# A third buffer for the scan's decay rows, four ScalarE operations held behind others, and other PSUM banks and an early Silu table at the entry of the second layer

## The chip, the cores and the metric

The kernel runs on one core of a Trainium2 chip. The metric is the device time of one execution in microseconds (us). Three executions of the kernel before took 1940.17, 1943.55 and 1943.87 us; their median is 1943.55 us. The profiled execution is a fourth one: it took 1941.21 us, of which 1939.4 us lie between its first and its last instruction (its span). All work is in float32; a matrix product that needs full precision is made of three products of a high and a low part of each factor.

## The reference, cut to what matters

One inference step of a trunk of two layers, for a prompt of 1024 positions and a sample group of 8 x 8 positions. The width is 1024. The first layer is a Mamba-2 SSD mixer with 8 groups of 4 heads, the second is a latent attention (MLA) over 16 heads with a Silu gate.

```python
def reference(...):
    for i in range(DEPTH):                       # DEPTH = 2
        ln = rms_norm(h, norm_w[i])
        if i % 2 == 0:                           # SSD: project, convolve, scan, gate, project
            out = ssd_mixer(ln, ...)
        else:                                    # MLA: project, attend, gate, project
            out = mla_output(o, gate, mla_w_out)
        h = h + out
    y = rms_norm(h, final_norm_w)

def ssd_scan(x, dt, a_head, bm, cm, init_state):   # chunks of 128 positions, per group
    a_cs = cumsum(dt * a_head)
    decay = where(causal, exp(a_cs[l] - a_cs[s]), 0)
    y_diag = einsum(cb * decay, x * dt)            # inside a chunk
    y_off = einsum(cc, state) * exp(a_cs)          # from the chunks before
    return y_diag + y_off, final_state

def mla_output(o, gate, w_out):
    return (o * silu(gate)) @ w_out
```

## The kernel before, in words

**Tiling.** The 1088 positions are nine row tiles: 0 to 7 with 128 prompt positions each, and 8 with the 64 sample positions. Activations that feed a projection are kept transposed as a high and a low part (`xh`, `xl` in the first layer, `hh`, `hl` in the second), eight slices of 128 channels each.

**First layer.** For each of the 8 groups g there are two pieces of work. The projection of group g (class `Group`, lines 481 to 572) makes four convolution blocks (`pj` in PSUM, `raw`, `acc`), applies Silu, and then the gates: nine products `pz` that ScalarE copies into `z`, a tile for row tiles 0 to 4 and another for 5 to 8, and Silu over each of them (lines 569, 571, 572). The scan of group g (`ssd_chunks`, lines 580 to 670) walks the nine row tiles. For each it loads the decay rows into a tile `M` of 128 x 4 x 128 by a DMA from `acs_d` (line 627), adds the causal mask on VectorE (line 628), takes four exponentials on ScalarE (line 631), multiplies with `cb` = B times C on VectorE (line 632), and multiplies with the transposed inputs `xsT` on TensorE (`py`, line 636). Beside it the states go on (`st`, `S`, `Ch`, `Sh`), and `ssd_states` handles the sample group in four further steps; it takes two tiles `xr` out of the same ring of buffers as `M` (line 688), and line 724 copies part of the product `pv` into `yo`. The ring has two buffers.

The scan of group g runs beside the projection of group g + 1. The last scan, g = 7, has no next group and runs beside the output projection (`OutHalf`, `ssd_out`): the first half of the weights (`xh`, `xl` again, made from `wor`/`wraw` at lines 769 and 770), row tiles `yta` transposed to `ytpa`, split by ScalarE (`yha`, line 127) and VectorE (`yla`, line 133), and multiplied into `poa`. In names such as `M7_0`, `yha0` or `z70` the first digit of a scan tile is the group, the last one the row tile. The second half of the output projection is `pob`; its result is added into the rows `xrb` on VectorE (lines 851 and 853, the second for the sample tile).

**Entry of the second layer** (`mla_in`). The rows are scaled, transposed into `xtp` (line 268) in groups of three row tiles, and split into `hh` by ScalarE (line 273) and `hl` by VectorE (line 274). Beside the transposes the first two of eight gate blocks are projected (`gate_block`): `pj` gets 24 products per piece of positions, and ScalarE applies Silu into `gt` (line 972). The weights of a block are loaded by DMA, copied to `wgh` on ScalarE (line 127) and split into `wgl` on GpSimd (line 131); the ring of weights has three buffers. The PSUM tiles of the second layer come from a new pool, laid out in the order in which its tags are first used: `tr` (three banks, for `xtp`), `pj` (two), `y` (three). They lie over the banks of the first layer's pool, whose first banks are those of `pj`, which `pob` used last.

**The end.** `pieces` (lines 1891 to 1965) makes the last projection, adds it to the rows `h`, takes the sum of squares per row on ScalarE (line 1935 for the sample tile), joins the partial sums on VectorE (lines 1939 and 1949), scales by 1/1024 and adds epsilon (line 1950), takes the power -1/2 on GpSimd (line 1951) and scales the rows.

**What sets the order.** Almost the whole program is written in a natural order, and a list scheduler with a model of the chip's times puts the instructions of each engine into a fixed order, so a constraint or a buffer more at one place can move instructions at others. `tc.issue_after(x)` tells it that what follows is to come after instruction x. The heads of the attention and what follows on TensorE and GpSimd have an order written by hand. Each engine takes its own instructions strictly in the order that stands in the program, and a wait holds up all that is behind it on that engine.

## Time and profile before

| what | value |
|---|---|
| time, three runs | 1940.17, 1943.55, 1943.87 us (median 1943.55) |
| profiled execution | 1941.21 us, span 1939.4 us, mean granted TensorE clock 0.996 |
| TensorE busy | 1895.6 us, 98% of the span |
| VectorE, ScalarE, GpSimd busy | 1192.2 us (61%), 1109.9 us (57%), 837.5 us (43%) |
| table loads of ScalarE for the decay rows (line 631) | 28, 1.28 us each |

In a row of the timeline stand start and length in us, engine, line, operation, output and inputs, and in brackets the idle time of the engine ahead of it with what ended it; the length runs from the first start to the last end of the merged instructions. In a row of the waits stand who waited for whom, the sum in us, the number of waits and the longest. In a row of a stretch stand, for each engine, busy time and number of instructions, then the granted TensorE clock (1.00 is full), the share of the DMA engines and their rate.

### The profile page before, as it was taken

The page shows a single profiled execution, that of the slowest core. Times are in us where ns is not written, and L with a number is a line of the kernel's source. Part 1 is how long each engine was busy: PE and PEld are TensorE (multiplying, and loading weights), DVE is VectorE, ACT ScalarE, POOL GpSimd, SP SyncE. Part 2 cuts the span into 40 slices and gives each one's busy share as a digit, 9 for nine tenths or more (in the row PEclk, how much of TensorE's full clock was granted, in tenths as well). Part 3 has the DMA queues.
Part 4 walks back from the last instruction along what each step waited for, and adds up shares of the span by engine and source line. Part 5 has one row for each costly group of instructions (what it writes and reads, how often), then busy time and mean ns, then how long its engine had stood idle before and what let it go on. Part 6 is the DMA issues. An engine that isn't in the chain of part 4 may idle for free.

```text
span 1939.4 us, 33638 instructions
## 1 busy us (share of the span) xinstructions
PE 1895.6 (98%) x12023; PEld 1730.3 (89%) x12023; DVE 1192.2 (61%) x2501; ACT 1109.9 (57%) x2535; POOL 837.5 (43%) x1122
## 2 busy tenths in 40 slices
PE   9999999999999999899999999999999999899998
PEld 7999999999999999788787998898888888788887
DVE  5567666656666666765533104476887888766674
ACT  6467666666666676732214314336777777855552
POOL 2446565555655555443003212103443334764551
PEclk9999999999999999999999999999999999989999
DMA  5123323332323332544433333133111112654431
GB/s 168 47 72 89 98 82 94 83 108 85 97 81 96 86 93 88 193 157 159 179 116 118 123 152 94 56 107 96 47 51 41 51 41 59 215 167 155 156 128 39
DMA packets 181087, 202.02 MB, mean 104 GB/s; under 512 B 18828, under 2 KB 147608, under 8 KB 180536
## 3 DMA queue, kind: packets, MB, share of 16 engines
q1 hardware_dynamic: 175864, 180.08, 30.1%
q0 software_dynamic: 4976, 19.66, 3.0%
q8 instruction: 95, 1.56, 0.3%
q14 instruction: 72, 0.59, 0.1%
q10 hardware_dynamic: 80, 0.13, 0.0%
HBM read 146.52 MB, written 53.28 MB: 103 GB/s over the span
## 4 chain that ended last, share of the span: by engine, by line
PE 88%; DVE 3%; DMA 3%; ACT 3%; issue 1%; POOL 1%; SPq 0%; POOLq 0%; DVEq 0%; ACTq 0%
PE pj L86 21%; PE pz L98 9%; PE pq L98 6%; PE pob L98 5%; PE p L98 5%; PE poa L98 4%; PE py L636 3%; PE sc L86 3%; PE o L86 2%; PE sc L1369 2%; PE o L1432 2%; PE o L1434 2%; PE st L1401 2%; PE st L1402 2%; PE st L1403 2%; PE o L1433 2%
## 5 line engine op out<-in xcount | busy, mean ns | idle before, releaser
L86 PE MATMUL pj<-xh,wih 128*128 128x384 f32 (+1 forms) x768 | 254.2, 335 | 0.9 <-ACT xh L273 0.5
L86 PE MATMUL pj<-xl,wih 128*128 128x384 f32 (+1 forms) x768 | 254.0, 331 | 0.0
L86 PE MATMUL pj<-xh,wil 128*128 128x384 f32 (+1 forms) x768 | 253.2, 330 | 0.0
L1415 POOL TENSOR_TENSOR tl<-P,th 128x384 fp32r<-128x384 f32 (+1 forms) x96 | 90.6, 944 | 232.5 <-ACT P L1413 190.9
L526 DVE SCALAR_TENSOR_TENSOR acc<-raw,vec,acc 128x1112 f32<-128x1112 f32 x96 | 141.6, 1476 | 25.9 <-ACT acc L522 24.9
L86 PEld LDWEIGHTS pj<-xh,wih 128*128 128x128 f32 x768 | 143.9, 188 | 2.5 <-ACT xh L273 1.1
L86 PEld LDWEIGHTS pj<-xl,wih 128*128 128x128 f32 x768 | 144.5, 188 | 1.0
L86 PEld LDWEIGHTS pj<-xh,wil 128*128 128x128 f32 x768 | 144.4, 188 | 0.5
L98 PE MATMUL pz<-wih,xh 128*128 128x256 f32 x504 | 142.9, 287 | 0.9 <-ACT z L567 0.8
L98 PE MATMUL pz<-wil,xh 128*128 128x256 f32 (+1 forms) x504 | 140.4, 285 | 0.9 <-DVE wil L133 0.9
L1412 ACT ACTIVATE th<-st 128x512 fp32r<-128x512 f32 x192 | 94.6, 493 | 66.0 <-PE st L1408 50.3
L631 ACT ACTIVATE M<-M,tok 128x128 f32<-128x128 f32 (+1 forms) x288 | 91.0, 386 | 67.2 <-DVE M L628 66.9
L98 PE MATMUL pz<-wih,xl 128*128 128x256 f32 x448 | 128.2, 286 | 0.0
L1705 POOL TENSOR_TENSOR kvl<-pgr,kvh 128x256 fp32r<-128x256 f32 x128 | 96.5, 781 | 60.5 <-ACT kvh L1703 60.3
L98 PEld LDWEIGHTS pz<-wih,xh 128*128 128x128 f32 x504 | 96.0, 190 | 2.0 <-ACT z L567 1.3
L98 PEld LDWEIGHTS pz<-wil,xh 128*128 128x128 f32 (+1 forms) x504 | 92.7, 184 | 1.7 <-DVE wil L133 1.1
L1413 ACT ACTIVATE P<-st 128x512 f32<-128x512 f32 x192 | 93.5, 487 | 0.0
L628 DVE TENSOR_TENSOR M<-M,negu 128x512 f32<-128x512 f32 x64 | 53.2, 831 | 65.5 <-DMA M<-acs_d 65.1
L613 POOL TENSOR_TENSOR xdd<-xsT,tok 128x256 f32<-128x256 f32 x64 | 50.4, 788 | 84.1 <-ACT xsT L599 84.0
L133 DVE TENSOR_TENSOR wil<-wraw,wih 128x512 fp32r<-128x512 f32 x88 | 72.0, 825 | 23.6 <-ACT wih L127 20.4
L98 PEld LDWEIGHTS pz<-wih,xl 128*128 128x128 f32 x448 | 85.3, 190 | 0.1
L1415 DVE TENSOR_TENSOR tl<-P,th 128x512 fp32r<-128x512 f32 x96 | 70.7, 737 | 18.9 <-ACT P L1413 18.7
(832 smaller groups left out, 6299.0 us busy)
## 6 DMA issues: line engine op xcount, KB each, us to landing
wraw<-in_ssd_w_in SPq DMA_DIRECT2D x92, 256.0 KB
M<-acs_d SPq DMA_DIRECT2D x64, 256.0 KB
s<-in_state_ssm SPq DMA_DIRECT2D x32, 256.0 KB
y_d<-y SPq DMA_DIRECT2D x64, 128.0 KB
out_s_ssm<-s SPq DMA_DIRECT2D x32, 256.0 KB
wraw<-in_ssd_w_out SPq DMA_DIRECT2D x12, 512.0 KB
q_d<-qt SPq DMA_DIRECT2D x32, 192.0 KB
qp<-q_d SPq DMA_DIRECT2D x8, 768.0 KB
```

The lines of the kernel that those rows point to most:

```text
L86: nc.tensor.matmul(out, a, b, start=(i == 0), stop=(i == n - 1))
L98: nc.tensor.matmul(o, a, b, start=(j == 0), stop=(j == len(ops) - 1))
L133: return (eng or nc.vector).tensor_tensor(lo, src, hi.bitcast(F32), op=ALU.subtract)
L526: last = nc.vector.scalar_tensor_tensor(acc, raw[:, j : j + n], k.convw[j][:, blk : blk + 1], acc, op0=ALU.mult, op1=ALU.add)
L613: nc.gpsimd.tensor_tensor(v3(xdd), v3(xsT), hb(2), op=ALU.mult)
L628: nc.vector.tensor_tensor(M[:m, :, :m], M[:m, :, :m], (k.negs if smp else k.negu)[:m, :m].unsqueeze(1).to_broadcast([m, 4, m]), op=ALU.add)
L631: nc.scalar.activation(M[:m, h, :m], M[:m, h, :m], AF.Exp, bias=tk[:, 0, 4 * g + h : 4 * g + h + 1])
L636: nc.tensor.matmul(py[:m, h * 64 : h * 64 + 64], M[:m, h, :m], xsT[:m, h * 64 : h * 64 + 64], start=True, stop=True)
L1412: nc.scalar.activation(th[:, :n], ps[:, :n], AF.Exp, scale=SCALE)
L1413: nc.scalar.activation(P[:, :n], ps[:, :n], AF.Exp, scale=SCALE)
L1415: eng.tensor_tensor(tl[:, :n], P[:, :n], th[:, :n].bitcast(F32), op=ALU.subtract)
L1705: nc.gpsimd.tensor_tensor(rl[:, j], raw[:, j], rh[:, j].bitcast(F32), op=ALU.subtract)
```

## The change

Eight edits, which belong together in five groups:

1. The ring of buffers that holds `M` and `xr` in the scan gets three buffers (`bufs=3`).
2. Four operations of ScalarE are held behind others: in the projection of group 7, the Silu over `z70` behind the last copy into `yo` that stands before it; in the scan of group 7, the four exponentials of row tile 0 behind the last copy of the split of `ytpa`; the weight copies of gate blocks 3 and 4 behind the Silu of the third pieces of gate blocks 0 and 1.
3. At the entry of the second layer the Silu table is loaded by an instruction of its own ahead of the gate blocks.
4. The second layer's PSUM pool is opened with a tile of tag `y` first, so that `y` gets the first three banks, `tr` the next three and `pj` the last two.
5. For the sample tile at the end, the scale of 1/1024 goes into the square on ScalarE (by a scale of 1024 to the power -1/2), and epsilon into the addition at line 1939, so that line 1950 falls away there.

```diff
@@ def split
-    nc.scalar.copy(hi, src)
+    k.cast = nc.scalar.copy(hi, src)
@@ Group.gates
             if i == 4:
-                nc.scalar.activation(z, z, AF.Silu)
+                with k.tc.issue_after(k.yoc.ins) if g == G - 1 else nullcontext():
+                    nc.scalar.activation(z, z, AF.Silu)
@@ ssd_chunks
-        M = sp.tile([128, 4, 128], F32, tag="M", name="M" + tag, bufs=2)
+        M = sp.tile([128, 4, 128], F32, tag="M", name="M" + tag, bufs=3)
...
-        for h in range(4):
-            nc.scalar.activation(M[:m, h, :m], M[:m, h, :m], AF.Exp, bias=...)
+        with k.tc.issue_after(k.ycast.ins) if g == G - 1 and i == 0 else nullcontext():
+            for h in range(4):
+                nc.scalar.activation(M[:m, h, :m], M[:m, h, :m], AF.Exp, bias=...)
@@ ssd_states
-        xr = sp.tile([128, 4, 128], F32, tag="M", name=f"xr3{tag}{q}", bufs=2)[:, :3, :96]
+        xr = sp.tile([128, 4, 128], F32, tag="M", name=f"xr3{tag}{q}", bufs=3)[:, :3, :96]
...
-            nc.scalar.copy(yr, pv[32:64, :128])
+            k.yoc = nc.scalar.copy(yr, pv[32:64, :128])
@@ OutHalf.prep
             split(k, yh[:, qs, :m], yh[:, qs, 64:] if m == 64 else yl[:, qs], pv)
+            k.ycast = k.cast
@@ gate_block
-    ws = kslices(load_w(...), 8)
+    with k.tc.issue_after(k.gts[5].ins) if b in (3, 4) else nullcontext():
+        ws = kslices(load_w(...), 8)
...
-        k.nc.scalar.activation(gt[:, t0 : t0 + n], p[:, :n], AF.Silu)
+        k.gts.append(k.nc.scalar.activation(gt[:, t0 : t0 + n], p[:, :n], AF.Silu))
@@ mla_in
+            k.gts = []
+            tc.keep_in_program_order(nc.scalar.preload_act_table_set("silu_and_others"))
@@ pieces
-                    nc.scalar.activation(junk[:, c], h[:m, c], AF.Square, accum_out=ss[:m, hf : hf + 1])
+                    nc.scalar.activation(junk[:, c], h[:m, c], AF.Square, scale=D**-0.5, accum_out=ss[:m, hf : hf + 1])
...
-                        nc.vector.tensor_tensor(ss[:m, 0:1], ss[:m, 0:1], ss[:m, 1:2], op=ALU.add)
+                        nc.vector.tensor_scalar(ss[:m, 0:1], ss[:m, 0:1], ss[:m, 1:2], EPS, op0=ALU.add, op1=ALU.add)
...
-            nc.vector.tensor_tensor(r, ss[:m, 0:1], ss[:m, len(cs) - 1 : len(cs)], op=ALU.add)
-            nc.vector.tensor_scalar(r, r, 1.0 / D, EPS, op0=ALU.mult, op1=ALU.add)
+            if src:
+                nc.vector.tensor_tensor(r, ss[:m, 0:1], ss[:m, 2:3], op=ALU.add)
+            else:
+                nc.vector.tensor_tensor(r, ss[:m, 0:1], ss[:m, 1:2], op=ALU.add)
+                nc.vector.tensor_scalar(r, r, 1.0 / D, EPS, op0=ALU.mult, op1=ALU.add)
@@ layer_mla
+        k.psum.tile([128, 512], F32, tag="y", name="y2", bufs=PB["y"])
```

Since the order is the scheduler's, the edits move instructions elsewhere too. Three places follow. In the rows the digits after a tile's name are numbers of buffers; line numbers of the changed kernel are up to eleven higher than before.

ScalarE where the last scan begins, before: the second table load here is for the exponentials of the first decay tile of group 7.

```order
L571 ACTIVATE z75_10203<-z75_10203 128x768
L127 CAST Ch7_1_10550<-acc70_9057 128x128
L667 COPY fo6_7_10200<-pf6_7_10197 128x256
L599 COPY xsT6_8_10263<-trp6_8_10260 64x256
L631 ACT_TABLE_LOAD
L631 ACTIVATE M7_0_10410<-M7_0_10410,tok_73 128x128
L109 COPY z75_10203<-pz_10344 64x256
L631 ACTIVATE M7_0_10410<-M7_0_10410,tok_73 128x128 x3
L127 CAST yha0_10328<-ytpa00_10330 128x512
L660 ACTIVATE xD6_7_10163,yssq_72<-y6_7_10190 128x256
L127 CAST yha0_10328<-ytpa01_10337 128x512
```

The same place in the change:

```order
L572 ACTIVATE z75_10203<-z75_10203 128x768
L127 CAST yha0_10328<-ytpa00_10330 128x512
L127 CAST yha0_10328<-ytpa01_10337 128x512
L633 ACT_TABLE_LOAD
L633 ACTIVATE M7_0_10410<-M7_0_10410,tok_73 128x128 x4
L662 ACTIVATE xD6_7_10163,yssq_72<-y6_7_10190 128x256
L109 COPY z75_10203<-pz_10344 64x256
L600 COPY xsT7_0_10394<-trp7_0_10390 128x256
L127 CAST BTh7_0_10396<-trp7_0_10390 128x128
L127 CAST xddh7_0_10402<-xdd7_0_10400 128x256
```

Both copies `yha0` now stand ahead of the table load and of the four exponentials of `M7_0`, which stood ahead of them.

VectorE some 15 us later in the last scan, before, from the split `sl7_800` of the first sample state to the split of the transposed B of row tile 1 (`xl` are the low parts of the last two weight slices):

```order
L133 TENSOR_TENSOR sl7_800_10465<-s0p7_800_10459,sh7_800_10464 128x512
L770 SCALAR_TENSOR_TENSOR xl_99<-wraw_10382,vec_154,xh_98 128x8x128
L731 TENSOR_TENSOR s07_800_10457<-s07_800_10457,sn7_800_10480 128x512
L133 TENSOR_TENSOR yla1_10519<-ytpa10_10520,yha1_10518 128x512
L628 TENSOR_TENSOR M7_1_10562<-M7_1_10562,negu_69 128x512
L770 SCALAR_TENSOR_TENSOR xl_99<-wraw_10386,vec_154,xh_98 128x8x128
L725 TENSOR_TENSOR yo7_10438<-yo7_10438,pv7_800_10468 32x128
L628 TENSOR_TENSOR M7_2_10647<-M7_2_10647,negu_69 128x512
L133 TENSOR_TENSOR yla1_10519<-ytpa11_10527,yha1_10518 128x512
L816 TENSOR_SCALAR yta3_10867<-yta3_10867,yrsa_10319 128x256 x4
L133 TENSOR_TENSOR BTl7_1_10541<-trp7_1_10534,BTh7_1_10540 128x128
```

The same stretch in the change:

```order
L133 TENSOR_TENSOR sl7_800_10465<-s0p7_800_10459,sh7_800_10464 128x512
L629 TENSOR_TENSOR M7_2_10647<-M7_2_10647,negu_69 128x512
L733 TENSOR_TENSOR s07_800_10457<-s07_800_10457,sn7_800_10480 128x512
L629 TENSOR_TENSOR M7_3_10809<-M7_3_10809,negu_69 128x512
L133 TENSOR_TENSOR yla1_10519<-ytpa10_10520,yha1_10518 128x512
L727 TENSOR_TENSOR yo7_10438<-yo7_10438,pv7_800_10468 32x128
L133 TENSOR_TENSOR yla1_10519<-ytpa11_10527,yha1_10518 128x512
L634 TENSOR_TENSOR M7_1_10562<-M7_1_10562,cb7_1_10560 128x512
L772 SCALAR_TENSOR_TENSOR xl_99<-wraw_10382,vec_154,xh_98 128x8x128
L634 TENSOR_TENSOR M7_2_10647<-M7_2_10647,cb7_2_10645 128x512
L818 TENSOR_SCALAR yta3_10867<-yta3_10867,yrsa_10319 128x256 x4
L772 SCALAR_TENSOR_TENSOR xl_99<-wraw_10386,vec_154,xh_98 128x8x128
```

The last `xl` stood in the fifth row behind `sl7_800`; it now stands in the eleventh, behind the decay tiles 1 to 3 and the four scalings of `yta3`.

TensorE at the entry of the second layer, the last product `pob` of the first layer and the first transposes and products of the second, with the semaphores that each waits for. Before:

```order
L98 MATMUL pob_12435<-woh_11536,yhb_12368 128x512
L268 MATMUL xtp_0_12484<-ident,xt_11842 128x128 [waits DVE_49,PE_49]
L268 MATMUL xtp_0_12484<-ident,xt_11924 128x128
L268 MATMUL xtp_0_12484<-ident,xt_12006 128x128
L268 MATMUL xtp_1_12490<-ident,xt_11842 128x128
```

In the change:

```order
L98 MATMUL pob_12435<-woh_11536,yhb_12368 128x512
L268 MATMUL xtp_0_12486<-ident,xt_11842 128x128
L268 MATMUL xtp_0_12486<-ident,xt_11924 128x128
L268 MATMUL xtp_0_12486<-ident,xt_12006 128x128
L268 MATMUL xtp_1_12492<-ident,xt_11842 128x128
```

The order is the same; the first transpose no longer waits for VectorE.

More of the change, by code (lines that the diff above doesn't have):

```diff
@@ L629, in ssd_chunks @@
                                 (k.negs if smp else k.negu)[:m, :m].unsqueeze(1).to_broadcast([m, 4, m]), op=ALU.add)
-        for h in range(4):
-            nc.scalar.activation(M[:m, h, :m], M[:m, h, :m], AF.Exp, bias=tk[:, 0, 4 * g + h : 4 * g + h + 1])
+        with k.tc.issue_after(k.ycast.ins) if g == G - 1 and i == 0 else nullcontext():
+            for h in range(4):
+                nc.scalar.activation(M[:m, h, :m], M[:m, h, :m], AF.Exp, bias=tk[:, 0, 4 * g + h : 4 * g + h + 1])
         nc.vector.tensor_tensor(M[:m, :, :m], M[:m, :, :m],
@@ L967, in gate_block @@
 def gate_block(k, wp, raws, b):
-    ws = kslices(load_w(k, wp, k.I["mla_w_in"][0][:, 800 + 128 * b : 928 + 128 * b], 8, 128, "wg", 3, raws, eng=k.nc.gpsimd, sub=4), 8)
+    with k.tc.issue_after(k.gts[5].ins) if b in (3, 4) else nullcontext():
+        ws = kslices(load_w(k, wp, k.I["mla_w_in"][0][:, 800 + 128 * b : 928 + 128 * b], 8, 128, "wg", 3, raws,
+                            eng=k.nc.gpsimd, sub=4), 8)
     gt = wp.tile([128, T], F32, tag="gt", name=f"gt{b}", bufs=2)
     def ev(ci, t0, n, p):
-        k.nc.scalar.activation(gt[:, t0 : t0 + n], p[:, :n], AF.Silu)
+        k.gts.append(k.nc.scalar.activation(gt[:, t0 : t0 + n], p[:, :n], AF.Silu))
     for ci in range(3):
```

## The prediction

> **What bounds the kernel now.** I read the page's busy line, then the stretches of the span, then TensorE's waits in the stretches that lose time, and last the instructions around those waits. First the page and the stretches (TensorE's busy time is the second number of a row, the clock stands ahead of the last two):

> ```profile
> PE 1895.6 (98%) x12023; PEld 1730.3 (89%) x12023; DVE 1192.2 (61%) x2501; ACT 1109.9 (57%) x2535; POOL 837.5 (43%) x1122
> ...
> 40.00:770.00 730.00, 723.05 (x5239) 705.87 (x5238) 465.17 (x760) 477.12 (x1155) 403.18 (x590) 1.00 0.30 85
> 770.00:850.00 80.00, 73.32 (x487) 64.69 (x486) 53.84 (x100) 50.15 (x114) 35.97 (x48) 0.98 0.57 189
> 1035.00:1085.00 50.00, 46.34 (x274) 40.83 (x273) 20.43 (x39) 26.12 (x49) 25.54 (x34) 1.00 0.46 150
> 1640.00:1720.00 80.00, 67.92 (x409) 58.95 (x408) 58.62 (x118) 58.37 (x120) 61.06 (x72) 0.94 0.64 200
> 1918.00:1940.00 22.00, 13.89 (x94) 12.06 (x92) 11.71 (x35) 3.81 (x10) 1.08 (x2) 0.91 0.12 36
> ```

> TensorE is busy in 1895.6 of 1939.4 us and its instructions stay the same in number and kind, so only its 44 us of idle time and its slow stretches can change. The edits reach four stretches: groups 0 to 6 of the scan (40 to 770, idle 7.0 us), the last scan (770 to 850, 6.7), the entry of the second layer (1035 to 1085, 3.7) and the end (8.1). The 12.1 us idle at 1640 to 1720 lie in code that is not touched. TensorE's waits in the last scan and around it:

> ```profile
> PE poa L98 <- ACT yha L127: 1.5, 1, 1.5
> PE pv L722 <- DVE sl L133: 1.3, 2, 1.1
> PE cb L625 <- DVE yo L725: 1.0, 1, 1.0
> PE poa L98 <- DVE xl L770: 0.9, 1, 0.9
> PE pz L98 <- ACT z L567: 0.8, 1, 0.8
> PE st L86 <- DVE BTl L133: 0.6, 1, 0.6
> PE st L86 <- ACT xddh L127: 0.3, 1, 0.3
> PE st L86 <- POOL xddl L133: 0.2, 1, 0.2
> ```

> **The entry of the second layer.** These rows carry it, TensorE's first, then those of VectorE, ScalarE and GpSimd:

> ```profile
> 1042.60 1.17 PE L268 MATMUL xtp<-ident,xt 128*128 128x128 f32 x9 [1.59 <-DVE xrb L853]
> 1056.58 0.45 PE L86 MATMUL pj<-hh,wgh 128*128 128x384 f32 x1 [0.77 <-ACT gt L972]
> 1079.59 0.44 PE L86 MATMUL pj<-hh,wgh 128*128 128x384 f32 x1 [1.16 <-ACT gt L972]
> ...
> 1041.77 0.69 DVE L853 TENSOR_TENSOR xrb<-xrb,pob 64x512 f32<-64x512 f32 x1
> 1043.86 1.67 DVE L274 SCALAR_TENSOR_TENSOR hl<-xtp,vec,hh 128x384 fp32r<-128x384 f32 x3 [1.40 <-ACT hh L273]
> 1035.51 1.98 ACT L127 CAST wgh<-wraw 128x1024 fp32r<-128x1024 f32 x2
> 1036.62 5.59 POOL L131 TENSOR_TENSOR wgl<-wraw,wgh 128x256 fp32r<-128x256 f32 x8 [0.18 <-ACT wgh L127]
> 1054.74 1.28 ACT L972 ACT_TABLE_LOAD   x1
> 1056.04 0.87 ACT L972 ACTIVATE gt<-pj 128x384 f32<-128x384 f32 x2
> 1078.15 1.04 ACT L127 CAST wgh<-wraw 128x1024 fp32r<-128x1024 f32 x1 [2.58 <-PE pj L86]
> 1079.10 0.43 ACT L972 ACTIVATE gt<-pj 128x320 f32<-128x320 f32 x1
> ```

> Banks: the first transposes sat 1.59 us until line 853 had emptied the bank of `pob`. In the change they wait for nothing, so they start when `pob` ends, 1042.60 - 1.59 = 1041.01. What is late next is `hl`: on VectorE it stands behind line 853, which still ends at 1041.77 + 0.69 = 1042.46. `hl` started at 1043.86 and could start at 1042.5, and the fourth transpose waits for it. So 1.4 of the 1.6 us are gained. Table: ScalarE's load of 1.28 us stood ahead of the first `gt`, and TensorE waited 0.77 for that `gt`. The load moves to 1035.5, ahead of the weight copies `wgh`. These then end at 1035.51 + 1.98 + 1.28 = 1038.8, and the first product, 1.4 earlier than now, comes at about 1042.5; GpSimd's split ends at 1043.5 instead of 1042.2 and is used slice by slice until 1054. So the load is hidden and the 0.77 is gained; without that cover it would cost up to its 1.28. Weight copies: at 1078.15 ScalarE copied a weight first and came to `gt` 0.95 later, and TensorE waited for that `gt`. In the change both `gt` go ahead: 0.95 gained. The weights of blocks 3 and 4 are then two `gt` (some 0.8) later, and are needed only after block 2, 72 products of over 0.16 us, which covers it. Together 1.40 + 0.77 + 0.95 = 3.1 us, between 2.3 (banks worth 0.6, if `hh` is late too) and 3.5 (all three waits).

> **The end.** Line 1950 goes from the chain behind the last product:

> ```profile
> 1933.52 0.15 DVE L1949 TENSOR_TENSOR ss<-ss 64x1 f32<-64x1 f32 x1 [0.57 <-ACT sq L1935]
> 1933.71 0.15 DVE L1950 TENSOR_SCALAR ss<-ss 64x1 f32<-64x1 f32 x1
> ```

> From start to start that is 0.19, so 0.2 us. The scale of the square and the second addition ride in instructions that run anyway.

> **The last scan.** Three waits are aimed at. (a) `cb` for `yo`, 1.0: the table load and Silu of `z70` stood ahead of the copy `yo`; now `yo` goes first. (b) `poa` for `yha`, 1.5:

> ```profile
> 799.26 0.69 DVE L628 TENSOR_TENSOR M<-M,negu 128x512 f32<-128x512 f32 x1 [1.35 <-DMA M<-acs_d]
> 801.69 0.59 ACT L127 CAST yha<-ytpa 128x512 fp32r<-128x512 f32 x1
> ...
> 802.00:803.00 1.00, 0.67 (x3) 0.53 (x4) 1.00 (x2) 1.00 (x4) 0.41 (x1) 0.89 1.14 326
> 803.00:804.00 1.00, 1.00 (x4) 0.70 (x3) 0.81 (x2) 0.98 (x2) 0.00 (x0) 0.50 0.87 345
> 805.00:806.00 1.00, 1.00 (x4) 0.81 (x3) 0.04 (x1) 1.00 (x2) 0.00 (x0) 0.50 1.00 303
> 806.00:807.00 1.00, 1.00 (x5) 0.77 (x5) 1.00 (x1) 1.00 (x5) 0.74 (x1) 0.91 0.86 311
> ```

> The decay tile came late by DMA, its exponentials with it, and `yha` stood behind them. In the change `yha` goes first. (c) The granted clock after that wait: 0.89, three times 0.50 and 0.91 in five microseconds, 0.11 + 1.5 + 0.09 = 1.7 us lost. Gross: 1.0 + 1.5 + 1.7 = 4.2 us. The 0.8 of `pz` stays but for some 0.2.

> [...] The rows above show the half rate right behind a gap of 1.5, so I count it; the gap of 1.59 at 1042 was not followed by one in its stretch, so a gap of this size is a draw.

> What speaks against the gross figure is what comes next. The four waits for `sl`, `xl`, `BTl` and `xddh` that follow at 815 to 825 are waits for VectorE and ScalarE working through their lists, and the change does not shorten these lists: the table loads there are as many as before. It also reorders them. Durations on VectorE:

> ```profile
> 816.62 1.27 DVE L770 SCALAR_TENSOR_TENSOR xl<-wraw,vec,xh 128x1024 fp32r<-128x1024 f32 x1
> 822.35 1.97 DVE L816 TENSOR_SCALAR yta<-yta,yrsa 128x256 f32<-128x256 f32 x4
> 825.63 0.67 DVE L632 TENSOR_TENSOR M<-M,cb 128x512 f32<-128x512 f32 x1
> ```

> Before, from the end of `sl7_800` to the last `xl` VectorE had two `xl` and three operations of 0.67, 4.5 us. In the change it has seven of 0.67 (two masks, two products, two `yla`, one state), one `yo` of about 0.3, `yta3` and two `xl`: 4.7 + 0.3 + 2.0 + 2.5 = 9.5 us. In the same stretch TensorE has about 5.7 us of work before it needs that `xl` (transposes of row tiles 1 and 2, `py` of both, eight `poa`, from the order with some 0.1 to 0.25 each), against 3.3 before. So it waits some 3.8 us there, where before it waited 0.9 and another 1.1 for `BTl`, `xddh` and `xddl`: 1.8 lost. An earlier weight slice is late too: a table load of 1.28 and the four exponentials of `M7_1`, about as long, now stand ahead of its copy on ScalarE, 2.6 us. TensorE may have other work for none or all of that; I take half, 1.3. Net 4.2 - 1.8 - 1.3 = 1.1 us gained. The ends: 4.4 (the lists hold nothing up, and the 0.2 of `pz`) and -4.5 (losses of 2.7 and 2.6, and two new slow stretches of 1.7 against the gross 4.2).

> **Groups 0 to 6.** A third buffer lets a decay tile be fetched before the tile two steps back is used up. It would remove waits such as this:

> ```profile
> PE pv L722 <- ACT sh L127: 1.3, 1, 1.3
> ```

> There `sh` stood on ScalarE behind exponentials whose tile came late. But the scheduler has used the buffer to move each tile one place forward: in groups 1 to 6 ScalarE's `M_6` now stands just ahead of that `sh` where `M_5` stood, and with three buffers the DMA of `M_6` is released by the same product `py_4` that released `M_5` with two. The distance to the DMA is as short as before. What is left is ten table loads less of 1.28 us on ScalarE, at the end of groups 1 to 6, where ScalarE keeps no one waiting for long. I take 0.6, between -1.5 (as much new idle as a fifth of the old) and 3.5 (half of the 7.0).

> **Sum.** 3.1 + 0.2 + 1.1 + 0.6 = 5.0 us. The profiled execution took 1941.21 (1.8 beside its span), so one like it would take 1936.2. The three runs shown have a median of 1943.55, 2.3 higher, but one of 1940.17: these four scatter around 1942.2, and I take the sum from there: **1937.2 us**. What a measurement of this kernel can tell from no change is about 0.2%, 3.9 us.

> **The rivals.**
> - *All is kept.* The lists of VectorE and ScalarE hold nothing up and the decay tiles come early in all groups: 3.5 + 0.2 + 4.4 + 3.0 = 11.1, 1931.1 us. For it: every wait aimed at is one instruction in front of another. Against: the lists are not shorter. 0.15.
> - *The last scan gives it back, the buffer does nothing.* Net -2 in the last scan, 0 in groups 0 to 6: 3.1 + 0.2 - 2 = 1.3, 1940.9 us. For it: the waits of 3.8 counted above and the releases that stay. 0.22.
> - *Slower.* The waits of the last scan grow into gaps that take the clock down again and again. The stretch 1640 to 1720 shows what such an episode is worth: 12.1 us idle at a mean clock of 0.94, which is another 4. If `poa` waits for its weight slices three times by 2 us and each gap draws a slow stretch of 1.7, that is 11.1 against a gross 4.2 and 2.0 of old waits: 4.9 lost; to come out 0.2% slower it takes 3.9 + 3.3 = 7.2 lost, so four such gaps, which lose 8.6: 1942.2 - 3.3 + 8.6 = 1947.5 us. For it: the reordered list. Against: TensorE has other work between most of these products. 0.08.
> - *Forecast*, 1933.5 to 1939.5: 0.55.

> **How the numbers follow.** Faster by over 0.2% (below 1938.3 from 1942.2, 1939.7 from the median): all of the first rival and 0.51 of the forecast, 0.66. Within 0.2%: the second rival and the rest of the forecast, 0.26. Slower: 0.08. The range leaves out the slow case and the far end of the first rival: 1931.5 to 1942.5.

> **What would show it.** The first `xtp` without a wait and `hl` starting 1.4 us after `pob`'s end; no table load between `hh` and `gt`; `gt` ahead of `wgh`; one operation less between the last square and GpSimd's power. In the last scan no wait of `poa` for `yha` and of `cb` for `yo`; clock 1.00 there; but waits of `poa` for `xl` or `xh`, and of the transposes for `yla`, of 3 us and more in all. In groups 0 to 6 the same idle time of 6 to 7 us. The forecast is wrong if idle time in 770 to 850 falls below 3 us or rises above 9, or if another stretch than these four moves by more than 2.

## The result, and the profile after

| | before | changed |
|---|---|---|
| median of six runs | 1942.59 us | 1933.62 us |
| lowest and highest | 1940.17, 1943.87 | 1931.64, 1939.72 |
| ratio | 1 | 0.9956, interval 0.9942 to 0.9969 |

The change makes the kernel 9.0 us faster, where 5.0 were summed. In a second session, with another profile, the ratio was 0.9944 (0.9925 to 0.9963). The first profiled execution of the changed kernel happens to be the slowest of its six, 1939.72 us, so its span (1937.9, before 1939.4) must not be taken for the result. Two executions among those of the experiments below (2291 us with the entry alone, 6886 us without the buffer) were in a slow state; the ratios leave them out, the printed medians do not.

The totals do not tell where the time went. So the program is cut where TensorE has issued the same number of its instructions (some 5500, 6250, 7000, 7250, 10750 and 11250): up to the last scan, the last scan, the output projection with what is left of the scan, the entry of the second layer, the attention (580.5 and 580.6 us, left out below), and the stretch that the prediction calls 1640 to 1720. Where the order of the products differs, such a cut is good to about 1 us. First the kernel before, the view of stretches:

```profile
0.00:758.30 758.30, 747.27 (x5343) 725.31 (x5344) 479.12 (x789) 494.41 (x1179) 406.73 (x610) 1.00 0.32 91
758.30:876.50 118.20, 111.52 (x729) 98.51 (x727) 78.17 (x147) 68.23 (x169) 53.60 (x74) 0.99 0.50 164
...
1025.80:1072.00 46.20, 43.70 (x248) 36.82 (x246) 19.53 (x34) 22.58 (x43) 19.65 (x25) 1.00 0.42 127
...
1652.50:1744.60 92.10, 80.86 (x481) 69.77 (x479) 62.53 (x125) 63.33 (x127) 67.34 (x83) 0.94 0.60 188
```

The same stretches in the first profile of the changed kernel:

```profile
0.00:753.00 753.00, 742.62 (x5335) 724.75 (x5336) 492.13 (x790) 486.34 (x1173) 394.62 (x608) 1.00 0.32 92
753.00:874.30 121.30, 112.92 (x733) 98.97 (x731) 80.93 (x148) 68.11 (x170) 57.56 (x77) 0.99 0.49 161
...
1022.40:1065.90 43.50, 42.95 (x244) 36.65 (x243) 19.52 (x34) 22.72 (x43) 19.59 (x25) 1.00 0.45 131
...
1646.50:1743.90 97.40, 84.82 (x487) 73.62 (x486) 64.24 (x129) 63.40 (x127) 67.11 (x83) 0.91 0.56 179
```

Behind the bounds of a stretch stand its length and TensorE's busy time. Up to the last scan 5.3 us are gained, in the last scan 3.1 lost, in the output projection 1.2 gained (149.3 to 148.1, row left out), at the entry 2.7 gained, and 5.3 lost in the last row, whose code is not touched. That last row is chance: in the second profile of the changed kernel it is 90.6 long.

The cut between the last scan and the output projection needs a caution: the row of the kernel before holds eight short products `py`, 0.8 us, that the others do not hold, or not all of them. Measured to the first product `pob` instead, up to which all have done the same work within half a microsecond, the changed kernel takes 2.4 us longer in its first profile and as long as before in its second (179.8, then 182.2 and 179.6).

The prediction had counted the stretch of the last row as constant, and had named a move of more than 2 us in such a stretch as a sign that it was wrong. That sign is no use here. In the twelve profiles of the experiments, whatever the kernel, the same products take between 89.8 and 97.6 us, at a granted clock of 0.91 to 0.96. That spread of 7.8 is nearly as wide as the spread of the six runs above, 8.1.

TensorE's waits in and around the last scan (784 to 842) in the first profile of the changed kernel, who waited for whom, sum, number, longest:

```profile
PE trp L595 <- DVE yla L133: 2.0, 1, 2.0
PE poa L98 <- ACT xh L771: 1.5, 1, 1.5
PE poa L98 <- DVE z L110: 1.3, 1, 1.3
PE poa L98 <- DVE xra L854: 0.8, 1, 0.8
PE poa L98 <- DVE xl L772: 0.6, 1, 0.6
```

The waits of `poa` for `yha` and of `cb` for `yo` are gone, as the change intends. In their place stand those that the prediction named: transposes for `yla`, products `poa` for the weight slices `xh` and `xl`, together 4.1 us. Those of `poa` for `z` and `xra` were not named.

The entry of the second layer in the same profile, timeline:

```profile
1033.14 1.28 ACT L1009 ACT_TABLE_LOAD   x1
...
1038.14 0.39 PE L98 MATMUL pob<-woh,yhb 128*128 128x512 f32 x1
1038.37 1.15 PE L268 MATMUL xtp<-ident,xt 128*128 128x128 f32 x9
1040.68 0.55 PE L268 MATMUL xtp<-ident,xt 128*128 128x128 f32 x3 [0.45 <-DVE hl L274]
...
1040.01 1.67 DVE L274 SCALAR_TENSOR_TENSOR hl<-xtp,vec,hh 128x384 fp32r<-128x384 f32 x3
...
1073.28 0.77 ACT L977 ACTIVATE gt<-pj 128x320 f32<-128x320 f32 x2 [2.60 <-PE pj L86]
1073.93 2.00 ACT L127 CAST wgh<-wraw 128x1024 fp32r<-128x1024 f32 x2
...
1073.77 0.45 PE L86 MATMUL pj<-hh,wgh 128*128 128x384 f32 x1 [0.23 <-ACT gt L977]
```

The first transposes follow `pob` without a wait. The Silu table is loaded 5 us ahead of them, where ScalarE had nothing else, and both `gt` stand ahead of the weight copies. What is late next is `hl`, for 0.45.

### The profile page after: what moved, and what is told of

Same layout as the page of the kernel before. It is cut to its first block, busy times and chain, and to the rows that moved or that the text cites. A ratio compares the mean times of both kernels' runs of the same rounds, so it can differ in the third digit from the quotient of the medians.

```text
span 1937.9 us, 33631 instructions
## 1 busy us (share of the span) xinstructions
PE 1894.9 (98%) x12023; PEld 1733.7 (89%) x12023; DVE 1209.1 (62%) x2500; ACT 1100.4 (57%) x2525; POOL 828.6 (43%) x1122
## 4 chain that ended last, share of the span: by engine, by line
PE 87%; DMA 4%; ACT 3%; DVE 3%; issue 1%; POOL 1%; SPq 0%; POOLq 0%; DVEq 0%; ACTq 0%
PE pj L86 24%; PE pz L98 7%; PE pq L98 6%; PE pob L98 5%; PE p L98 5%; PE poa L98 3%; PE py L638 3%; PE sc L86 3%; PE o L86 2%; PE sc L1376 2%; PE o L1439 2%; PE o L1441 2%; PE st L1408 2%; DMA M<-acs_d 2%; PE st L1409 2%; PE st L1410 2%
## 5 line engine op out<-in xcount | busy, mean ns | idle before, releaser
L86 PE MATMUL pj<-xl,wih 128*128 128x384 f32 (+1 forms) x768 | 255.4, 333 | 0.0
L86 PE MATMUL pj<-xh,wih 128*128 128x384 f32 (+1 forms) x768 | 252.9, 333 | 0.5 <-ACT raw L512 0.3
L86 PE MATMUL pj<-xh,wil 128*128 128x384 f32 (+1 forms) x768 | 252.9, 329 | 0.0
L1422 POOL TENSOR_TENSOR tl<-P,th 128x384 fp32r<-128x384 f32 (+1 forms) x96 | 90.6, 944 | 232.3 <-ACT P L1420 190.6
L98 PE MATMUL pz<-wih,xh 128*128 128x256 f32 x504 | 143.4, 288 | 2.5 <-ACT z L567 2.5
L86 PEld LDWEIGHTS pj<-xh,wih 128*128 128x128 f32 x768 | 143.8, 188 | 1.9 <-ACT xh L273 0.7
L86 PEld LDWEIGHTS pj<-xl,wih 128*128 128x128 f32 x768 | 144.5, 188 | 1.0
L86 PEld LDWEIGHTS pj<-xh,wil 128*128 128x128 f32 x768 | 144.4, 188 | 0.5
L98 PE MATMUL pz<-wil,xh 128*128 128x256 f32 (+1 forms) x504 | 139.6, 283 | 0.0
L98 PE MATMUL pz<-wih,xl 128*128 128x256 f32 x448 | 128.9, 288 | 0.0
L133 DVE TENSOR_TENSOR wil<-wraw,wih 128x512 fp32r<-128x512 f32 x88 | 74.2, 849 | 40.7 <-ACT wih L127 34.0
L98 PEld LDWEIGHTS pz<-wih,xh 128*128 128x128 f32 x504 | 95.9, 190 | 3.5 <-ACT z L567 2.9
L98 PEld LDWEIGHTS pz<-wil,xh 128*128 128x128 f32 (+1 forms) x504 | 92.8, 184 | 0.3
L98 PEld LDWEIGHTS pz<-wih,xl 128*128 128x128 f32 x448 | 85.3, 190 | 0.5
L127 ACT CAST wih<-wraw 128x512 fp32r<-128x512 f32 x92 | 55.9, 616 | 43.9 <-PE pj L86 28.9
```

The lines of the kernel that those rows point to most:

```text
L86: nc.tensor.matmul(out, a, b, start=(i == 0), stop=(i == n - 1))
L98: nc.tensor.matmul(o, a, b, start=(j == 0), stop=(j == len(ops) - 1))
L127: k.cast = nc.scalar.copy(hi, src)
L133: return (eng or nc.vector).tensor_tensor(lo, src, hi.bitcast(F32), op=ALU.subtract)
L1422: eng.tensor_tensor(tl[:, :n], P[:, :n], th[:, :n].bitcast(F32), op=ALU.subtract)
```

## The experiments

Each kernel was timed against the kernel before on the same chip, and left one profile. A ratio here has an interval 4 to 8 us wide, so it tells whether an edit does something; where it does it is read from the stretches, cut as above.

### The third buffer alone

```diff
-        M = sp.tile([128, 4, 128], F32, tag="M", name="M" + tag, bufs=2)
+        M = sp.tile([128, 4, 128], F32, tag="M", name="M" + tag, bufs=3)
-        xr = sp.tile([128, 4, 128], F32, tag="M", name=f"xr3{tag}{q}", bufs=2)[:, :3, :96]
+        xr = sp.tile([128, 4, 128], F32, tag="M", name=f"xr3{tag}{q}", bufs=3)[:, :3, :96]
```

> The kernel before with one edit: three buffers instead of two for the tiles M and xr of the scan. Theory of the prediction (T): the scheduler spends the buffer by moving every tile one place forward, so groups 0 to 6 gain 0.6 us and the last scan, without the two holds, about nothing: 0 to 1 us below the kernel before. Rival (B): the buffer is the main part of the measured gain of 9; the last ctp, which ends the projection of group 7, starts at 761.0 in the profile after and at 764.9 before, 3.9 earlier: 4 us or more below the kernel before, and the last ctp at 760 to 762. Rival (C): what the buffer gives, it gives only together with the holds: 0 here.

Measured: 1934.48 us, ratio 0.9956 (0.9939 to 0.9973), 8.5 us below the kernel before by the ratio; the last `ctp` starts at 762.5. The theory of the prediction falls: the buffer alone gives about as much as the whole change. The stretches put it in groups 0 to 6 (755.0 against 758.3 up to the last scan) and in the last scan (115.9 against 118.2).

### The entry alone

```diff
+    with k.tc.issue_after(k.gts[5].ins) if b in (3, 4) else nullcontext():
+        ws = kslices(load_w(...), 8)
...
+            tc.keep_in_program_order(nc.scalar.preload_act_table_set("silu_and_others"))
...
+        k.psum.tile([128, 512], F32, tag="y", name="y2", bufs=PB["y"])
```

> The kernel before with the three edits at the entry of the second layer alone: the early Silu table, the weight copies of gate blocks 3 and 4 behind the gt, the tile of tag y first in the PSUM pool. Theory (T): 3.1 us below the kernel before (2.3 to 3.5), as the profile after shows it there (from the last pob at 1040.6 to the first pk at 1154.3 before 113.7 us, after 1038.1 to 1148.6 is 110.5: 3.2). Rival: the shift of what follows is worth another 3 to 6 us, since later stretches (1640 to 1720 with its 12 us idle and a clock of 0.94) fall otherwise: 6 us or more.

Measured: 1938.33 us, ratio 0.9974 (0.9958 to 0.9990), between 1.9 and 8.2 us. The profile has 44.0 us at the entry against 46.2, 2.2 gained, at the low end of the range given. The ratio's middle, 5, would need more than that. But this profile is also 0.9 shorter up to the last scan and 0.8 in the output projection, where the order of the work is that of the kernel before: so much two executions of the same order differ. 2 to 3 us are shown, and the interval does not exclude more.

### The two holds alone

```diff
+                with k.tc.issue_after(k.yoc.ins) if g == G - 1 else nullcontext():
+                    nc.scalar.activation(z, z, AF.Silu)
...
+        with k.tc.issue_after(k.ycast.ins) if g == G - 1 and i == 0 else nullcontext():
+            for h in range(4): ...
```

> The kernel before with the two holds of the last scan alone (Silu of z70 behind the copy yo, exponentials of M7_0 behind the casts yha), two buffers. Theory (T): the two waits of 1.0 and 1.5 go and with them the slow stretch of 1.7, and 3.1 come back in waits of poa; net 1.1 below the kernel before. Rival (K): most of the losses counted (the xl in the 11th row of VectorE) come from the third buffer, which lets M7_1 to M7_3 go ahead; with two buffers nothing comes back: 3.5 to 4.4 below. Rival (N): nothing at all, 0, because VectorE's and ScalarE's lists are as long.

Measured: 1941.91 us, ratio 0.9990 (0.9979 to 1.0002). The last scan takes 116.0 us against 118.2: 2.2 gained, between the theory's 1.1 and the rival's 3.5. Both waits aimed at are gone, but `poa` waits 1.8 for `xl`, and a stretch of 3.4 us at half rate follows that wait (from 819.38) just as one followed the old (from 802.77). The ratio alone does not tell this kernel from the one before.

### The change without the buffer

> The changed kernel with two buffers again, all other edits kept. Theory (T): 0.6 us above the changed kernel, so some 8 below the kernel before. Rival (B): the buffer is worth 4 us or more, so 4 to 5 below the kernel before. Rival (C): the holds need the buffer: 3 to 3.5 below the kernel before, the entry and the end alone.

The edit is the first diff of this section, undone in the changed kernel. Measured: 1936.60 us, ratio 0.9961 (0.9948 to 0.9973): 7.6 below the kernel before. Read as a difference, the buffer would be worth 1 us here and 8.5 us in the first experiment. The parts do not seem to add: 8.5 + 5.1 + 1.9 is 15.5, and the whole is 9, or 10.9 by the ratio of the second session. With intervals this wide that is a hint and no more: something in the change may work against the buffer. The stretches say where to look. Length of the last scan, one profile each:

| | without holds | with both holds |
|---|---|---|
| two buffers | 118.2, 118.6 | 116.0, 116.5 |
| three buffers | 115.9 | 121.3 |

Each edit by itself gains 2.2 or so; together they lose 3.1 in this profile.

### The changed kernel again

> The changed kernel once more, for a second profile and a time beside the next three. In its first profile the stretch from the 5500th to the 6250th instruction of TensorE, the last scan, took 121.3 us (753.0 to 874.3; before 118.2, the buffer alone 115.9, the holds alone 116.0). Theory (L): the loss there comes from the order, so this profile shows it again, 120 to 122. Rival (O): that profile was one bad execution, since it took 1939.72 against 1931.6 to 1936.1 of the other five; here 115 to 118. The untouched stretch 1640 to 1720 may take 90 to 97 in either case.

Measured: 1932.72 us, ratio 0.9944 (0.9925 to 0.9963); last scan 118.8 us. That lies between the two expectations: part of the 121.3 was chance (the waits of `poa` for `z` and `xra` are 0.3 in all instead of 2.1), but with 118.8 there is still no gain in the last scan. The stretches of this profile:

```profile
0.00:753.50 753.50, 743.35 (x5340) 725.38 (x5341) 492.14 (x791) 485.97 (x1173) 393.13 (x609) 1.00 0.32 92
753.50:872.30 118.80, 114.01 (x728) 99.08 (x727) 78.09 (x148) 67.95 (x169) 56.26 (x76) 0.97 0.50 164
...
1021.40:1064.60 43.20, 42.65 (x243) 36.47 (x242) 19.51 (x34) 22.71 (x43) 19.57 (x25) 1.00 0.44 129
...
1644.60:1735.20 90.60, 80.34 (x481) 69.27 (x480) 63.46 (x127) 63.16 (x128) 68.52 (x83) 0.96 0.62 192
```

This execution (1931.93 us) is near the median, and its gain of 9.2 us (1939.4 to 1930.2) splits so, one execution against one: 4.8 up to the last scan, -0.6 in it, 0.2 in the output projection (149.3 to 149.1), 3.0 at the entry, 0.5 in the attention, 1.5 in the untouched stretch, and -0.2 behind it.

### Without both holds, without each

Three kernels, each the changed kernel with one or both of these undone:

```diff
-                with k.tc.issue_after(k.yoc.ins) if g == G - 1 else nullcontext():
-        with k.tc.issue_after(k.ycast.ins) if g == G - 1 and i == 0 else nullcontext():
```

Without both:

> The changed kernel without the two holds of the last scan: three buffers, the entry and the end. Theory (L): buffer and holds harm each other in the last scan, so without the holds it is 4 to 5 us below the changed kernel, some 12 below the kernel before; the last scan as with the buffer alone, 115 to 117 us. Rival (O): the holds cost nothing; the same as the changed kernel within 1.5 us.

Without the hold of the exponentials of `M7_0`, and the same kernel once more in the next session:

> The changed kernel without the hold of the exponentials of M7_0; the Silu of z70 is still held behind yo. If the hold of the exponentials does the harm (it is what lets the exponentials pile up with those of M7_1 ahead of the weight copies), 3 to 5 us below the changed kernel and equal to the kernel without both holds; if the hold of the Silu does, as the changed kernel.

> The changed kernel without the hold of the exponentials of M7_0 once more, beside the run before, for a second measurement and profile of it: 1928 to 1931 if the first one was typical. Its last scan (5500th to 6250th instruction of TensorE) took 116.5 us in the first profile; 115 to 118 again if the hold is what cost 2 to 4 there, 119 and more if that was chance.

Without the hold of the Silu of `z70`:

> The changed kernel without the hold of the Silu of z70; the exponentials of M7_0 are still held behind yha. The mirror of the run before: as the changed kernel if the hold of the exponentials does the harm, 3 to 5 us below it if the hold of the Silu does.

| | time, us | ratio | last scan, us |
|---|---|---|---|
| changed kernel | 1932.72 | 0.9944 (0.9925 to 0.9963) | 118.8 (121.3 in the first profile) |
| without both holds | 1930.33 | 0.9935 (0.9915 to 0.9955) | 116.8 |
| without the hold of `M7_0` | 1929.56 | 0.9928 (0.9911 to 0.9945) | 116.5 |
| the same again | 1928.89 | 0.9935 (0.9918 to 0.9953) | 115.2 |
| without the hold of `z70` | 1933.75 | 0.9944 (0.9926 to 0.9962) | 119.0 |

In the last scan the answer is clear: every kernel that shares three buffers with `xr` and holds `M7_0` needs 118.8 or more, every one that shares them and does not hold it (the buffer alone too, 115.9) 116.8 or less, and the hold of `z70` makes no difference. In time it is about 3 us, the low end of what was expected. The ratios' intervals overlap, but the first, second, third and fifth kernel of the table ran in one session: there the twelve executions with the hold of `M7_0` have a median of 1933.5 us and the twelve without it 1929.6, and the means are 2.6 apart. Without this hold the kernel is faster than both kernels of the case.

How the hold costs in the changed kernel is seen on ScalarE. The changed kernel, second profile, timeline (table loads, exponentials, copies `yha` and `xh`):

```profile
792.39 1.06 ACT L127 CAST yha<-ytpa 128x512 fp32r<-128x512 f32 x2
793.47 1.28 ACT L633 ACT_TABLE_LOAD   x1
794.76 1.28 ACT L633 ACTIVATE M<-M,tok 128x128 f32<-128x128 f32 x4
...
798.48 1.28 ACT L573 ACT_TABLE_LOAD   x1
...
801.84 1.15 ACT L771 ACTIVATE xh<-wraw,vec 128x1024 fp32r<-128x1024 f32 x1 [1.24 <-DMA wraw<-in_ssd_w_out]
803.01 1.28 ACT L633 ACT_TABLE_LOAD   x1
804.30 1.28 ACT L633 ACTIVATE M<-M,tok 128x128 f32<-128x128 f32 x4
...
805.94 1.15 ACT L771 ACTIVATE xh<-wraw,vec 128x1024 fp32r<-128x1024 f32 x1
```

The same without the hold of `M7_0`, its second profile:

```profile
780.26 1.27 ACT L632 ACTIVATE M<-M,tok 128x128 f32<-128x128 f32 x4
...
794.94 1.07 ACT L127 CAST yha<-ytpa 128x512 fp32r<-128x512 f32 x2
...
796.80 1.15 ACT L770 ACTIVATE xh<-wraw,vec 128x1024 fp32r<-128x1024 f32 x1
...
799.44 1.15 ACT L770 ACTIVATE xh<-wraw,vec 128x1024 fp32r<-128x1024 f32 x1 [0.66 <-DMA wraw<-in_ssd_w_out]
...
805.05 1.28 ACT L632 ACT_TABLE_LOAD   x1
```

Without the hold the decay tile `M7_0` is there in time, and its exponentials run at 780.26, with the table that was loaded for group 6 at 776.21, long before `yha`. So the shared ring of three already removes the wait for `yha` that the hold was made for. The hold then puts them behind `yha`, at 794.76, into a stretch where ScalarE runs Silu: the loads at 793.47, 798.48 and 803.01 take the place of the one at 805.05. The second `xh` comes at 805.94 instead of 799.44, and this is what TensorE waits for, with what follows (timeline and stretches of the changed kernel, second profile):

```profile
807.14 1.18 PE L98 MATMUL poa<-xh,yha 128*128 128x512 f32 x2 [1.58 <-ACT xh L771]
```

```profile
807.50:813.50 6.00, 5.53 (x23) 4.23 (x22) 5.38 (x10) 2.64 (x8) 1.35 (x2) 0.50 0.43 148
```

Behind the wait of 1.58 the clock is at 0.50 for 6.8 us (807.22 to 814.04), which costs 3.4.

That is the way of this order, and not the reason in general. The kernel without the hold of `z70` keeps the hold of `M7_0` and needs 119.0 as well, but ScalarE has as few table loads as without the hold (22 for exponentials of decay tiles in the whole program, 23 in the changed kernel), its second `xh` comes at 800.33, and TensorE does not wait for `xh` at all. It waits for other operations that the scheduler moved back (784 to 842):

```profile
PE pv L723 <- DVE sl L133: 1.3, 1, 1.3
PE st L86 <- POOL xddl L133: 1.1, 1, 1.1
PE ytpa L825 <- DVE b L703: 1.0, 1, 1.0
PE st L86 <- ACT xddh L127: 1.0, 1, 1.0
```

Two stretches at half rate of 3.4 us each lie among these waits. So it is shown that the hold costs with this ring, and for each of the two orders which waits it costs; what is common to them is only that the hold made the scheduler choose another order.

### More room in the ring

If room for decay tiles is what counts in groups 0 to 6, the two `xr` of a group, which share the ring, should matter too.

```diff
-        xr = sp.tile([128, 4, 128], F32, tag="M", name=f"xr3{tag}{q}", bufs=...)[:, :3, :96]
+        xr = sp.tile([128, 3, 96], F32, tag="xr", name=f"xr3{tag}{q}", bufs=1)
```

In the kernel before, with two buffers for `M`:

> The kernel before with the tiles xr of the sample states in a ring of their own (one buffer of 128 x 3 x 96), while the decay rows M keep two buffers. The buffer alone was measured at 0.9956 of the kernel before, some 8.5 us less; of that, up to the 5500th instruction of TensorE, some 3.5 lie in groups 0 to 6 and 2.3 in the last scan. Theory (M): the decay tiles need the third buffer; here groups 0 to 6 gain 0 to 1 and the whole is 0 to 3 below the kernel before. Rival (X): what the third buffer removes is that the two xr of each group take the places of two decay tiles; then this does nearly as much: 5 us or more below.

In the kernel before, with three buffers for `M`:

> The kernel before with three buffers for the decay rows M and a ring of its own for xr (one buffer). Theory (M): as the third buffer alone, 7 to 10 us below the kernel before, since the third buffer is what counts. Rival (X): as the run before, whatever it gives. A further gain over the third buffer alone (more than 2 us) would say that both uses were short of room.

In the changed kernel without the hold of `M7_0`:

> A try at a faster version: the changed kernel without the hold of the exponentials of M7_0 (measured at 0.9928 of the kernel before, against 0.9944 for the changed kernel in the same session), and with xr in a ring of its own. If the room of xr matters, 2 us or more below that, 1927 or less; if not, 1928 to 1931.

Measured: 1941.78 (ratio 0.9990, 0.9979 to 1.0000), 1949.61 (1.0037, 1.0023 to 1.0050) and 1944.68 us (1.0008, 0.9995 to 1.0022). The time of the first is what was expected if the decay tiles need the third buffer, but its stretches are not: up to the last scan it needs 761.5 us, 3.2 more than the kernel before, and 115.8 in the last scan, 2.4 less. The other two agree with nothing that was expected: three buffers for `M` with `xr` apart are 16 us slower than three buffers shared with `xr`, by the ratios. Their last scans take 118.0 and 116.9 us without the hold of `M7_0`, and `poa` waits 1.8 and 1.6 for `yha` again: three buffers for `M` are not enough to remove that wait. Up to the last scan the three-buffer kernels need 753 to 755 us; with `xr` apart, in the second of the three kernels, the stretch and then TensorE's longest waits from 100 to 760:

```profile
0.00:767.60 767.60, 748.71 (x5340) 727.10 (x5341) 486.09 (x792) 499.99 (x1187) 406.91 (x609) 1.00 0.32 91
```

```profile
PE sn L729 <- DVE S L643: 5.8, 4, 2.2
PE cb L625 <- DVE yo L725: 3.3, 2, 2.4
```

TensorE is idle for 18.9 us there instead of 9 to 11. These waits are of the sample group. The single `xr` may pace its steps, and with two buffers for `M` the separation costs 3.2 us too; whether it is the single buffer or the separation was not tried, so these runs do not tell which tiles need the third buffer. What is shown is that room by itself does not make these groups faster.

## Why the prediction was right, and where it was not

The time, 1933.6, lies inside the range and at the edge of the forecast's own (1933.5 to 1939.5). The direction was right. But the sum, 5.0 against 9.0, came out as near as it did by luck, from two errors of opposite sign.

**The entry, 3.1 (2.3 to 3.5): right.** 2.7 and 3.0 in the two profiles, 2.2 alone. All three mechanisms show. `hl` starts 1.64 after the first transpose where 1.5 was worked out, and the fourth transpose waits 0.45 for it where the sum left 0.2: 1.14 of the 1.59 are gained, not 1.4. The wait of `pj` for `gt` at the first block, 0.77, is gone with its table load; at the second it is 0.23 instead of 1.16, so 0.93 gained, not quite the 0.95. Together that is 2.8.

**The end, 0.2: right.** From the start of the last addition to the start of GpSimd's power it was 0.51 before (1933.52 to 1934.03) and is 0.29:

```profile
1932.21 0.15 DVE L1957 TENSOR_TENSOR ss<-ss 64x1 f32<-64x1 f32 x1 [0.57 <-ACT sq L1942]
1932.50 0.54 POOL L1961 TENSOR_TENSOR ss<-ss,nhalf 64x1 f32<-64x1 f32 x1 [6.78 <-DVE ss L1957]
```

**The last scan, net 1.1 gained: wrong, no gain in either profile, mainly by one term.** VectorE, first profile, the stretch that was forecast to take 9.5 us:

```profile
810.42 0.68 DVE L133 TENSOR_TENSOR sl<-s0p,sh 128x512 fp32r<-128x512 f32 x1
...
819.79 1.63 DVE L772 SCALAR_TENSOR_TENSOR xl<-wraw,vec,xh 128x1024 fp32r<-128x1024 f32 x1
```

From the end of `sl` to the end of the last `xl` are 10.3 us (9.3 in the second profile), and TensorE's waits for `yla`, `xh` and `xl` sum to 4.1 and 3.8. The forecast had 3.8 of waits from VectorE's list and 1.3 from the table load and exponentials of `M7_1` ahead of an `xh`; the latter is the wait of 1.5 or 2.1, while `yla` and `xl` come to 2.6 and 1.7. So the new waits were some quarter smaller in sum than the 5.1, and idle time went about as it should: 6.7 us before, 8.4 and 4.8 after (length less busy time), on average the same. The step that failed is (c) of the gross gain, "0.11 + 1.5 + 0.09 = 1.7 us lost", booked as gained. The half rate goes with one wait and comes with another: it costs 1.7 before, 1.7 again in the first profile and 3.4 in the second (what the clock lacks to 1.00, summed over the stretch). The rest of the loss of 3.1 and 0.6 is 1.4 and 0.8 of other busy time (busy time less half rate is 109.8 before, 111.2 and 110.6 after), which is no more than the cuts leave uncertain.

That the holds were needed was a second error: the shared third buffer alone already takes away both waits (the wait of `cb` for `yo` is 0.2 in its profile, one of `poa` for `yha` is not there). The comparison of the two orders had only before and after in it, and could not tell which edit moved what.

**Groups 0 to 6, 0.6 (-1.5 to 3.5): the main error.** In seven profiles with the shared ring of three the products up to the last scan take 752.9 to 755.0 us, in four with the shared ring of two 757.4 to 758.3: some 4 gained, above the far end. The step that failed is the bound "half of the 7.0". It took TensorE's idle time for all that could be won. The idle time did stay where it was forecast (11.0 us before, 10.4 and 10.2 after); it is the busy time that fell, from 747.27 to 742.62 and 743.35, for the same products. Busy is not full speed: a product is shown longer than the time to the start of the next (0.28 against 0.12 below), and a product that starts late behind a short one, or a wait below some 0.15 us, hides in it. In the changed kernel, second profile, at one place:

```profile
561.80 0.27 PE L724 MATMUL pv<-sh,cblk 128*64 128x128 f32 x1
561.91 0.33 PE L98 MATMUL pz<-wih,xh 128*128 128x256 f32 x1
562.08 0.28 PE L98 MATMUL pz<-wil,xh 128*128 128x256 f32 x1
562.20 0.28 PE L98 MATMUL pz<-wih,xl 128*128 128x256 f32 x1
```

Behind the short `pv` the first `pz` holds TensorE for 0.17 us (561.91 to 562.08) instead of 0.12, and no wait is shown. And since a product of 0.28 is shown 0.16 longer than the distance to the next start, a wait below that leaves no idle time. Such late starts can be counted over the timeline up to the last `ctp`: starts with no wait shown that come more than 0.045 us later than is usual after the product ahead. How many there are depends on what is taken as usual. By three ways of counting, three profiles with the shared ring of three have 20 to 35 fewer than three with two buffers (some 380 against 405 by one of them), and they sum to 2 to 3 us less; no half rate falls into this stretch in these six. So about half or more of the 4 us are delays of this kind; the rest is spread too thinly over 5300 products to be told apart, and why the other order has fewer late starts stays open.

The argument behind the 0.6, that the scheduler spends the buffer and leaves the distance to the DMA as short as it was, is not refuted: ScalarE's waits for masked decay tiles are 55.9 us before and 52.4 after (100 to 760 and 756). What the buffer bought shows as another order on TensorE, which the prediction had no means to price. Another order can lose as well: with `xr` apart, three buffers gave one that is 9 us worse than before, though there the single `xr` acts too.

**The clock.** The half rate did follow gaps of 1 to 2 us here (1.51 before; 1.58 in the changed kernel, above), so counting the 1.7 was right in kind; the error was to think that it would not come again. That a gap of this size is a pure draw, as the prediction has it, is not borne out either: in the last section one and the same wait of 2.12 was followed by half rate in the three profiles where 1.93 us or more of it lay in one step of 3.41 us, and not in the four where it was spread over two. The first rival (all is kept, 1931.1) is nearer to the median than the forecast's 1937.2, but not for its reason: the 4.4 that it kept in the last scan were lost, and groups 0 to 6 gave more than its 3.0.

## What to carry to other kernels

Idle time bounds what removing the waits that are shown can give, but not what another order of the same instructions can give: compare the busy time of the same products as well. When a change fixes one wait in two ways, try each way alone; here the buffer let the exponentials go early, the hold made them late again, and a kernel without the hold is some 3 us faster. And look at the explanation in every run that should show it: the extra table loads explain the changed kernel, but not the kernel without the hold of `z70`, which is as slow there. Do not book the half rate behind a wait of 1 to 2 us as a gain when the wait goes, if other waits of that size take its place: here it cost 1.7 us in the last scan before, and 1.7 and 3.4 in the two profiles after.

## What the runs showed of the hardware

Within each of the fourteen profiles all changes of the clock lie whole multiples of 3.41 us apart (before: 1, 261, 2, 2, 1 and 65 times 3.41). In the two profiles of the kernel without the hold of `M7_0` they do not lie at the same times: the half rate in the last scan starts at 810.66 in one and at 812.47 in the other. Cut from these changes on into steps of 3.41 us, the profile of before and the first of the changed kernel have 1116 steps at full rate (the first 4 to 5 us and the last 14 left out). Six of them were followed by half rate; in these TensorE was idle for 1.51, 3.15 and 2.23 us before, and for 1.99, 3.09 and 3.00 us in the changed kernel. In the other 1110 it was idle for at most 1.76 us, so 1.51 was followed by half rate and 1.76 was not; what decides there stays open.

The length of a wait alone does not tell. A wait of `pz` for `z` of 2.12 us at 185 stands at the same place in all seven profiles with the shared ring of three, and the half rate follows in three of them and not in four. In the three, 1.93 to 2.12 us of idle time lie in one step; in the four the wait lies across the boundary of two steps, and the fuller step has 1.26 to 1.48. With the third buffer alone (the step with the wait, then the next; length less TensorE's busy time is idle):

```profile
184.86:188.27 3.41, 1.29 (x11) 1.25 (x11) 1.02 (x2) 3.39 (x10) 0.62 (x2) 1.00 0.05 19
188.27:191.69 3.42, 3.42 (x19) 3.42 (x18) 1.85 (x2) 2.15 (x9) 2.33 (x3) 0.50 0.11 38
```

The changed kernel, second profile, the two steps over which the same wait is spread:

```profile
182.58:185.99 3.41, 2.54 (x22) 2.31 (x21) 1.02 (x3) 3.38 (x7) 1.47 (x3) 1.00 0.43 109
185.99:189.41 3.42, 2.16 (x18) 2.16 (x19) 1.19 (x3) 3.41 (x12) 1.54 (x3) 1.00 0.00 0
```

The wait of 1.59 at the entry of the kernel before lay across such a boundary too (0.69 and 1.04 us idle in the two steps) and no half rate followed; in the kernel with three buffers and `xr` apart it lay in one step (1.69 idle), and half rate did follow (the entry took 47.3 us instead of 46.2).

In the untouched stretch two to five pieces of 3.4 us fall per profile, which cost 3.4 to 8.5 us. That is as wide as the gains looked for here, and a reason why the profile of a single execution cannot show a gain of 5 us in its total.
